# Gram products traced at the head of a step, and one PSUM group for branch B's output

## The chip, the cores and the metric

The kernel runs on one core of a Trainium2 chip. Its time is the device time of one execution in microseconds; it was taken in three runs, and the median counts. Five engines work side by side, each through its own list of instructions in a fixed order: TensorE (PE) multiplies, VectorE (DVE) and ScalarE (ACT) do elementwise work and copy results out of PSUM, GpSimd (POOL) does some of the elementwise work, and SyncE (SP) issues the DMAs. An instruction waits until what it reads has been written and what it overwrites has been read.

## The reference

One decoder block over 1040 tokens of width 1024 (16 meta tokens and 1024 of the sequence), all in float32: a half-step feed-forward (FFN1), two sequence mixers A and B on the same normalized input, their gated sum through an output projection, a second feed-forward (FFN2). This change concerns the mixers.

- A is a gated DeltaNet with 8 heads of width 128. In chunks of 64 tokens in the reference: `m = strict(kb @ k.T * decay)`, `tinv = inv(m + I)`, `u = tinv @ vb`, `wk = tinv @ (kb * exp(g))`, `attn = (q @ k.T) * decay`, and then a chain over the chunks, `v_new = u - w @ state`, `o = qg @ state + attn @ v_new`, `state = state * exp(gl) + kt.T @ v_new`.
- B is an RWKV-7 recurrence with 16 heads of width 64, token by token in the reference:

```
sa = einsum('bhvk,bhk->bhv', state, a_t)
state = state * w_t + sa * b_t + v_t * k_t
y_t = einsum('bhvk,bhk->bhv', state, r_t)
```

The kernel computes B in chunks too: products of decayed keys and queries inside a chunk (Gram products), the inverse of a triangular matrix, and a state handed from chunk to chunk. Then `o_a` and `o_b` are normalized, gated and added.

## The kernel before

The program has three parts: FFN1 (0 to some 790 us), the mixers (to some 2300 us), and the output projection with FFN2. The mixers run in 16 steps: two segments of tokens (528 with the meta tokens, then 512), in each eight steps j, and a step handles head j of A and heads 2j and 2j+1 of B. A head of B has 64 rows, so B's matmuls are 64x64 and use one quadrant of the PE array each; HS are the two halves of 64 rows.

What a step consists of, as functions: `decay`, `new_b` and `new_a` make the inputs of a later step by the input projection (the matmuls pp, L307, three for each weight tile w, whose halves ACT L163 and DVE L164 prepare). `operands` (L1411) makes the Gram products: B's grb (L1428), masked into LT by DVE (L1431), and A's gra (L1467), from which DVE takes UA (L1471) and attn (L1473). It then sends LT and UA's diagonal blocks through DRAM (scr, L1548 and L1551) and loads them in another layout as Ub (L1557, L1559); transposes keys (bkt, L1498, into BKt) and AR (vp<-ck,AR, into at); computes B's output inside a chunk from older tokens (vp<-LT,Vs, copied by ACT into yb, L1515); and makes ktl and the scaled kq. `inverses` (L1562) inverts the small diagonal blocks in 62 serial DVE instructions (tb L1581, Xb L1583), copies the result (Yt, L1584) and sends it through DRAM. `merge_blocks` builds the whole inverse Y of them (iv). `transitions` (L1645) solves with Y (xp), and makes B's chunk transitions: xa, xv, vbk, mt, AR's second half and vbk's final form, with the PSUM tiles xp, vp, mp and np; the second part of np (np<-LT,xv) is B's output from the solved values, which DVE adds to yb (L1698). `chains` (L1701) runs both chains over the chunks (p, b, pq) and ends with bq (L1773), B's output from the states; DVE adds it to yb (L1775). `gates` and `finish` (L1808) normalize and merge; cs and bon (L1213) are their sums over rows of hl.

PSUM has eight banks: four for pp (mm), two for the operands (mx), two for transitions, chains and bq (ch). A tile waits for a bank of its pool until what stood in it has been copied out.

The order comes from a table of strings (L187 to L192), which says in which order the functions are traced: "+" is a function of the next step, "++" of the one after. A scheduler then puts the instructions of each engine into a fixed order; it prefers what was traced earlier among what its model takes to be ready. The steps of one segment have the same order on each engine but for buffers. Helper `run` (L1249, matmul L1266) issues 16 matmuls for each kind that it is given, over all four quadrants, into two banks of a pool.

Of the kernel before, what the change touches and what calls it, by code (L numbers as in the profile page):

```python
# [25 lines left out]
FULL = 512  # L26
CB = 64
NCB = FULL // CB
CA = 128
NCA = FULL // CA  # L30
# [3 lines left out]
HS = (slice(0, 64), slice(64, 128))  # L34
# [149 lines left out]

FIRST = "decay new_b tokens new_a decay+ operands inverses new_b+ new_a+"  # L187
REGULAR = "merge_blocks transitions operands+ inverses+ chains gates finish decay++ new_b++ new_a++"
BEFORE_SWITCH = "merge_blocks transitions operands+ inverses+ chains gates finish banks gates+ segment decay++ new_b++ tokens++ new_a++"
SWITCH = "merge_blocks transitions operands+ inverses+ chains finish decay++ new_b++ new_a++"  # L190
LAST_BUT_ONE = "merge_blocks transitions operands+ inverses+ chains gates finish"
FINAL = "gates merge_blocks transitions chains fill finish"  # L192


# [858 lines left out]
def ch3(ap, c):  # L1053
    return ap.rearrange("p (a b) -> p a b", b=c)
# [184 lines left out]
def tok(i, h):  # L1239

    return h ^ (i & 1)


def key(i, h):

    return 1 - tok(i, h)


def run(g, pool, name, *kinds):  # L1249


    ps, out, used = {}, [], [0, 0]
    for f in kinds:
        ds = [f(i, 0)[2] ^ f(i, 0)[3] for i in range(2)]
        at = []
        for d in ds:
            if d not in ps:
                ps[d] = pool.tile([P, 512], F32, name=name, tag=pool.name)
            at.append(used[d])
            used[d] += NCB // 2 * CB  # L1260
        for i in range(NCB):
            e, c0 = ds[i & 1], at[i & 1] + i // 2 * CB
            for h in range(2):
                l, r, src, dst = f(i, h)
                assert src ^ dst == e
                g.nc.tensor.matmul(ps[e][HS[dst], c0 : c0 + CB], lhsT=l, rhs=r, start=True, stop=True)  # L1266
        out.append([(ch3(ps[d][:, c0 : c0 + NCB // 2 * CB], CB), cs) for d, c0, cs in zip(ds, at, EO)])
    return out
# [139 lines left out]
        nc.scalar.activation(vkm[:, 0, :], ps[:16, 0:P], AF.Copy)  # L1408


def operands(g, q):  # L1411

    nc, st, V, c, j, n, off = g.nc, g.st, g.V, q.c, q.j, q.n, q.off
    meta = q.s == 0
    fs = slice(off, off + FULL)
    tmp = lambda name, w=528: tmp_tile(g, name, w)
    kq, AR, BK = q.kq, q.AR, q.BK
# [4 lines left out]
    LT = q.LT = st.tile([P, NCB, 2, P], F32, name="LT", tag="LT", bufs=2)  # L1422
    for c4 in range(0, NCB, 4):
        ps = [g.mx.tile([P, 512], F32, name="grb", tag="mx") for _ in range(2)]
        for i in range(4):
            for d in range(2):
                for h in range(2):
                    nc.tensor.matmul(ps[d][HS[h ^ d], i * P : (i + 1) * P], lhsT=BK[HS[h], c4 + i, d ^ (i & 1)],  # L1428
                                     rhs=AR[HS[h], c4 + i].rearrange("p a b -> p (a b)"), start=True, stop=True)
# [3 lines left out]
    if meta:  # L1433
        nc.vector.tensor_copy(g.bkpm[0:64, 0, :], g.bkm[0:64, :])
        nc.vector.tensor_copy(g.bkpm[64:128, 1, :], g.bkm[64:128, :])
        ps = g.mx.tile([P, 512], F32, name="gbm", tag="mx")
        for h in range(2):
# [3 lines left out]
                                op=ALU.mult)  # L1441


    E = ch3(tmp("E", 512), CA)
    kts = st.tile([P, NCA], F32, name="kts", tag="kts")
# [9 lines left out]
    eg = gp  # L1455
    nc.scalar.activation(eg, gp, AF.Exp)
    nc.scalar.activation(kts, kts, AF.Exp)
    egl = q.egl = st.tile([P, NCA], F32, name="egl", tag="egl", bufs=2)
    nc.gpsimd.tensor_copy(egl.unsqueeze(2), ch3(eg, CA)[:, :, CA - 1 : CA])
    attn = q.attn = st.tile([P, NCA, CA], F32, name="attn", tag="attn", bufs=2)  # L1460
    UA = q.UA = st.tile([P, NCA, CA], F32, name="UA", tag="UA", bufs=1)
    for b in range(2):
        ps = g.mx.tile([P, 512], F32, name="gra", tag="mx")
        for c2 in range(2):
            i = 2 * b + c2
            tsl = slice(off + i * CA, off + (i + 1) * CA)
            nc.tensor.matmul(ps[:, c2 * 256 : c2 * 256 + 256], lhsT=kq[:, 0, tsl], rhs=kq[:, :, tsl],  # L1467
                             start=True, stop=True)
# [5 lines left out]
    if meta:  # L1474
# [3 lines left out]
        em = q.em = st.tile([16, 3, 16], F32, name="em", tag="em", bufs=2)  # L1478
# [10 lines left out]

    inverse_inputs(g, q)  # L1490

    BKt = q.BKt = st.tile([P, NCB, 2, CB], F32, name="BKt", tag="BKt")
    ident = g.C("ident")
    ps = [g.mx.tile([P, 512], F32, name="bkt", tag="mx") for _ in range(2)]
    for i in range(NCB):
        for d in range(2):
            for h in range(2):
                nc.tensor.matmul(ps[d][HS[h ^ d], i * CB : (i + 1) * CB], lhsT=BK[HS[h], i, d ^ (i & 1)],  # L1498
                                 rhs=ident[HS[h], HS[h]], start=True, stop=True)
    for d in range(2):  # L1500
        nc.scalar.activation(BKt[:, :, d], ch3(ps[d], CB), AF.Copy)

    Vs = q.Vs
    at = q.at = st.tile([P, NCB, CB], F32, name="at", tag="at")
    yb = q.yb = st.tile([P, FULL], F32, name="yb", tag="yb", bufs=2)

    def vr(i, h):
        k = key(i, h)
        return Vs[HS[k], i], LT[HS[k], i, 1 - (i & 1), CB:], k, h

    pa, pr = run(g, g.mx, "vp", lambda i, h: (AR[HS[h], i, 0, :], ident[HS[h], HS[h]], h, tok(i, h)), vr)
    for ps, cs in pa:
        nc.scalar.activation(at[:, cs], ps, AF.Copy)
    for ps, cs in pr:
        nc.scalar.activation(ch3(yb, CB)[:, cs], ps, AF.Copy)  # L1515
# [6 lines left out]
    ps = g.mx.tile([P, 512], F32, name="ktp", tag="mx")  # L1522
# [3 lines left out]
    if meta:  # L1526
        vkm = q.vkm
        ps = g.mx.tile([P, 512], F32, name="vmp", tag="mx")
# [76 lines left out]
def merge_blocks(g, q):  # L1605

    nc, st = g.nc, g.st
    LT, UA, Xc, XA = q.LT, q.UA, q.Xc, g.XA
    Y = g.Y[q.it % 2]
# [32 lines left out]
    nc.vector.tensor_copy(Y[0:64, NCB:, 64:128], ch3(ps4[0:64, 0:256], 64))  # L1642


def transitions(g, q):  # L1645

    nc, st = g.nc, g.st
    Y = g.Y[q.it % 2]
    AR, LT, BKt, Vs, yb = q.AR, q.LT, q.BKt, q.Vs, ch3(q.yb, CB)
    vbk = q.vbk = st.tile([P, NCB, CB], F32, name="vbk", tag="vbk")  # L1650
    xa, xv = (st.tile([P, NCB, CB], F32, name=x, tag=x) for x in ("xa", "xv"))

    vka = q.at
# [12 lines left out]

    def va(i, h):
        k = key(i, h)
        return LT[HS[k], i, 1 - (i & 1), :CB], Vs[HS[k], i], k, 1 - k

    def vb(i, h):
        k = key(i, h)
        return BKt[HS[k], i, 1 - (i & 1)], Vs[HS[k], i], k, h

    px, pv = run(g, g.ch, "xp", solved(q.at), va)
    for ps, cs in pv:
        nc.scalar.activation(vka[:, cs], ps, AF.Copy)
    for ps, cs in px:
        nc.scalar.activation(xa[:, cs], ps, AF.Copy)
    for ps, cs in run(g, g.ch, "xp", solved(vka))[0]:  # L1680
        nc.scalar.activation(xv[:, cs], ps, AF.Copy)
    for ps, cs in run(g, g.ch, "vp", vb)[0]:
        nc.scalar.activation(vbk[:, cs], ps, AF.Copy)
    bt = lambda r, i: BKt[r, i, i & 1]
    br = lambda r, i: LT[r, i, i & 1, CB:]
    pm, pr = run(g, g.ch, "mp", by_tok(lambda r, i: xa[r, i], bt), by_tok(lambda r, i: xa[r, i], br))
    for ps, cs in pm:
        for hp in HS:
            nc.vector.tensor_tensor(g.mt[hp, cs, hp], ps[hp], g.C("ident")[hp, hp].unsqueeze(1).to_broadcast([CB, NCB // 2, CB]),  # L1689
                                    op=ALU.add)  # L1690
    for ps, cs in pr:
        nc.vector.tensor_tensor(AR[:, cs, 1, :], ps, AR[:, cs, 1, :], op=ALU.add)
    pn, py = run(g, g.ch, "np", by_tok(bt, lambda r, i: xv[r, i]), by_tok(lambda r, i: xv[r, i], br))
    for ps, cs in pn:
        nc.vector.tensor_tensor(vbk[:, cs], ps, vbk[:, cs], op=ALU.add)
    nc.vector.tensor_tensor(vbk, vbk, q.gam.unsqueeze(2).to_broadcast([P, NCB, CB]), op=ALU.mult)
    for ps, cs in py:
        nc.vector.tensor_tensor(yb[:, cs], ps, yb[:, cs], op=ALU.add)  # L1698


def chains(g, q):  # L1701

    nc, st, c, j = g.nc, g.st, q.c, q.j
    meta = q.s == 0
# [6 lines left out]
    if meta:  # L1711
        ym, ltm, uvm = q.ym, q.ltm, g.uvm[q.it % 2]
        ps = pt("bm1")
# [4 lines left out]
        ps = pt("bm2")  # L1718
# [3 lines left out]
        ps = pt("bm3")  # L1722
# [4 lines left out]
        ps = pt("am1")  # L1727
# [3 lines left out]
        ps = pt("am2")  # L1731
# [27 lines left out]
    SBs = st.tile([P, NCB + 1, CB], F32, name="SBs", tag="SBs")  # L1759
# [9 lines left out]
        chunk_a(i)  # L1769
    ps = pt("bq")  # L1770
    for i in range(NCB):
        for hp in HS:
            nc.tensor.matmul(ps[hp, i * CB : (i + 1) * CB], lhsT=SBs[hp, i], rhs=q.AR[hp, i, 1, :],  # L1773
                             start=True, stop=True)
# [33 lines left out]
def finish(g, q):  # L1808
# [17 lines left out]
    else:  # L1826
        g.mg.append(u_tile(g, yb))


ACTIONS = {"new_b": new_b, "tokens": tokens, "new_a": new_a, "operands": operands, "inverses": inverses, "merge_blocks": merge_blocks, "transitions": transitions,  # L1830
           "chains": chains,
           "gates": gates, "finish": finish, "fill": fill}

# [85 lines left out]
```

## Time and profile before

| what | value |
|---|---|
| time, median of three runs | 3006.02 us (3003.01 to 3011.42) |
| the profiled execution | 3009.62 us, span 3007.6 us |
| mean granted PE clock | 0.99 of full speed |
| PE, DVE, ACT, POOL busy | 96%, 73%, 48%, 16% of the span |
| one step, first segment | 94.0 us, of which PE is busy 90.8 |
| one step, second segment | 86.9 us, of which PE is busy 83.8 |

A row of a timeline gives start, length, engine, source line, operation, output<-inputs, shapes and number of instructions; in brackets stand the idle time just before it and what ended it. A wait row says which engine and line waited for which, then the total in us, the number of times and the longest. A row by line gives number, busy time, mean ns of one, and idle time before. A 64x64 or 128x128 fp32 matmul is recorded as two instructions, so that 16 matmuls are 32 records; pp, whose operands are split into two halves beforehand, is one record each. Each time in the text is of the profiled execution unless the median is named.

### The profile page before, as it was taken

Reading aid. Unit: us, or ns where it says so; the run is one execution under the profiler, and the core shown is the slowest. Engines: PE = TensorE matmul, PEld = TensorE weight load, DVE = VectorE, ACT = ScalarE, POOL = GpSimd, SP = SyncE. Lnnn points to the kernel's source line nnn. Section 1 sums busy time; section 2 is a strip of 40 time slices with the busy share of each in tenths; the row PEclk is TensorE's granted clock in tenths of the full one; section 3 lists DMA queues with packets and bytes.
Section 4 is the critical chain, followed back from the end, with each engine's and each line's share of the span. In section 5 each row is a group of like instructions: output and inputs, shape, how many; then the busy total and the mean of one; then the engine's idle time right before and its main releaser. Section 6 shows DMA issues by size and latency. Waiting matters only on the chain.

```text
span 3007.6 us, 62829 instructions
## 1 busy us (share of the span) xinstructions
PE 2890.0 (96%) x25630; PEld 2501.7 (83%) x25630; DVE 2194.8 (73%) x4079; ACT 1445.0 (48%) x2546; POOL 491.2 (16%) x554
## 2 busy tenths in 40 slices
PE   8999999998989999999998999999998999999998
PEld 8999999998878888888776777777776888888886
DVE  7566668776667877788767887777866666667886
ACT  5322234345655656566566656656644432223444
POOL 0332332323000000000000100100100033332531
PEclk9999999999999999999999999999999999999999
DMA  3433236453232322333332332233354333333762
GB/s 123 134 107 106 93 122 210 170 193 111 74 74 66 83 72 64 81 82 87 93 90 71 81 82 75 74 84 86 106 148 158 114 109 103 100 104 132 248 226 95
DMA packets 286849, 333.14 MB, mean 111 GB/s; under 512 B 172432, under 2 KB 178576, under 8 KB 286560
## 3 DMA queue, kind: packets, MB, share of 16 engines
q1 hardware_dynamic: 284752, 325.77, 35.7%
q8 instruction: 201, 3.29, 0.5%
q10 hardware_dynamic: 1728, 3.16, 0.3%
q14 instruction: 88, 0.72, 0.1%
q0 software_dynamic: 80, 0.19, 0.0%
HBM read 261.67 MB, written 67.38 MB: 109 GB/s over the span
## 4 chain that ended last, share of the span: by engine, by line
PE 50%; DVE 12%; ACT 5%; issue 2%; DMA 1%; SPq 0%; POOL 0%; DVEq 0%; ACTq 0%
PE pp L307 16%; PE pg L494 11%; PE pd L707 6%; PE pwo L307 3%; DVE w L164 2%; DVE tb L1581 1%; PE pg L518 1%; DVE Xb L1583 1%; ACT w L163 1%; PE cs L1213 1%; PE vp L1266 1%; PE mp L1266 1%; DVE mt L1689 1%; PE gra L1467 1%; PE np L1266 1%
## 5 line engine op out<-in xcount | busy, mean ns | idle before, releaser
L307 PE MATMUL pp<-uk,w 128*128 128x512 f32 (+2 forms) x4824 | 969.8, 347 | 15.2 <-DVE h L714 6.0
L307 PEld LDWEIGHTS pp<-uk,w 128*128 128x128 f32 x4824 | 744.0, 191 | 111.9 <-DVE w L164 13.1
L707 PE MATMUL pd<-form,w 128*128 128x256 f32 (+2 forms) x2772 | 437.2, 320 | 9.9 <-DVE w L164 9.2
L707 PEld LDWEIGHTS pd<-form,w 128*128 128x128 f32 x2772 | 396.7, 190 | 49.9 <-DVE w L164 12.3
L494 PE MATMUL pg<-bt,w 128*128 128x256 f32 (+2 forms) x2520 | 401.7, 318 | 2.5 <-DVE w L164 2.0
L164 DVE TENSOR_TENSOR w<-wraw,w 128x1024 fp32r<-128x1024 f32 (+2 forms) x266 | 349.2, 1313 | 74.9 <-ACT w L163 71.8
L494 PEld LDWEIGHTS pg<-bt,w 128*128 128x128 f32 x2520 | 360.2, 188 | 36.4 <-DVE w L164 3.1
L163 ACT ACTIVATE w<-wraw 128x1024 fp32r<-128x1024 f32 (+2 forms) x266 | 276.5, 1040 | 191.5 <-PE pg L494 116.1
L500 DVE TENSOR_TENSOR c<-c,pg 128x520 f32<-128x520 f32 (+1 forms) x280 | 189.5, 689 | 240.0 <-PE pg L494 216.0
L494 PE MATMUL pg<-b,w 128*128 128x256 f32 (+2 forms) x2160 | 347.9, 318 | 0.0
L494 PEld LDWEIGHTS pg<-b,w 128*128 128x128 f32 x2160 | 309.8, 188 | 28.0
L163 ACT ACTIVATE w<-wrx 128x1024 fp32r<-128x1024 f32 (+1 forms) x64 | 58.4, 912 | 280.4 <-PE pg L494 238.5
L464 POOL TENSOR_TENSOR wrx<-wrx 128x512 f32<-128x512 f32 x38 | 52.5, 1382 | 727.0 <-DVE w22b L164 549.8
L164 DVE TENSOR_TENSOR form<-form 128x520 fp32r<-128x520 f32 (+1 forms) x152 | 145.1, 991 | 13.0 <-ACT form L163 12.7
L163 ACT ACTIVATE w<-wsum 128x768 fp32r<-128x768 f32 x96 | 75.7, 788 | 160.3 <-PE pd L707 120.9
L164 DVE TENSOR_TENSOR w<-wsum,w 128x768 fp32r<-128x768 f32 x96 | 116.0, 1214 | 36.8 <-ACT w L163 36.8
L1583 DVE TENSOR_TENSOR Xb<-Xb,tb 115x126 f32<-115x126 f32 (+22 forms) x496 | 125.8, 254 | 8.9 <-DVE tb L1581 0.2
L163 ACT ACTIVATE form<-form 128x520 fp32r<-128x520 f32 (+1 forms) x152 | 94.2, 632 | 77.1 <-DMA form<-frm 67.7
L1581 DVE TENSOR_TENSOR tb<-Ub,Xb 115x126 f32<-115x126 f32 (+22 forms) x496 | 124.5, 251 | 8.4 <-DMA Ub<-scr 1.2
L242 POOL TENSOR_TENSOR wsum<-wsum,wraw 128x768 f32<-128x768 f32 (+1 forms) x48 | 96.3, 2020 | 209.7 <-DMA wraw<-in_wdn 122.1
L1390 DVE SCALAR_TENSOR_TENSOR acc<-xr,pk,acc 128x528 f32<-128x528 f32 (+1 forms) x144 | 108.9, 757 | 28.5 <-ACT acc L1386 28.0
L307 PE MATMUL pwo<-uk,w 128*128 128x512 f32 x384 | 99.5, 412 | 4.1 <-DVE w L164 1.9
(424 smaller groups left out, 4391.3 us busy)
## 6 DMA issues: line engine op xcount, KB each, us to landing
wraw<-in_win SPq DMA_DIRECT2D x150, 512.0 KB
wraw<-in_wgu SPq DMA_DIRECT2D x44, 512.0 KB
wrx<-in_wgu SPq DMA_DIRECT2D x44, 512.0 KB
frm<-c SPq DMA_DIRECT2D x76, 260.0 KB
form<-frm SPq DMA_DIRECT2D x76, 260.0 KB
frm<-c SPq DMA_DIRECT2D x76, 256.0 KB
form<-frm SPq DMA_DIRECT2D x76, 256.0 KB
wraw<-in_wdn SPq DMA_DIRECT2D x40, 384.0 KB
```

The source lines that it names most:

```text
L163: g.nc.scalar.activation(hi, src, AF.Copy)
L164: (eng or g.nc.vector).tensor_tensor(lo, src, hi.bitcast(F32), op=ALU.subtract)
L242: g.nc.gpsimd.tensor_tensor(s, x, y, op=ALU.add if r == 1 else ALU.subtract)
L307: g.nc.tensor.matmul(ps, lhsT=l, rhs=r, start=i == 0, stop=i == n - 1)
L464: sums.tensor_tensor(a22, a21, a22, op=ALU.add)
L494: nc.tensor.matmul(ps[:, c0 : c0 + cn], lhsT=l[:, x, k, :], rhs=r[:, k, y, c0 : c0 + cn], start=i == 0, stop=i == 3 * HK - 1)
L500: nc.vector.tensor_tensor(o, x, y, op=ALU.add)
L707: nc.tensor.matmul(pd[:, c0 : c0 + cn], lhsT=wd[:, u, k - k0, :], rhs=x[:, v, c0 : c0 + cn], start=k + i == 0, stop=k == HF - 1 and i == 2)
L1266: g.nc.tensor.matmul(ps[e][HS[dst], c0 : c0 + CB], lhsT=l, rhs=r, start=True, stop=True)
L1390: nc.vector.scalar_tensor_tensor(acc[:, :n], xr[:, tap : tap + n], V("convw", ct * 4 + tap), acc[:, :n], op0=ALU.mult, op1=ALU.add)
L1581: nc.vector.tensor_tensor(tv, U[:, i, i + 1 :].unsqueeze(2).to_broadcast([npt, nt, ncc]), X[:, i, 0:ncc].unsqueeze(1).to_broadcast([npt, n ...
L1583: nc.vector.tensor_tensor(X[:, i + 1 :, 0:ncc], X[:, i + 1 :, 0:ncc], tv, op=ALU.add)
```

## The change

`operands` is cut into two functions. `grams` makes LT, the decay matrix E, attn and UA, em, and the inversion's loads; `operands` keeps BKt, at, ktl, the scaled kq and the state loads. In the table, the next step's `grams` stands at the head of a step, ahead of `merge_blocks` of the step itself; `operands` stays behind `transitions`. UA gets two buffers, yb one.

B's output is summed differently. The products vp<-LT,Vs in `operands` and np<-LT,xv in `transitions`, 16 matmuls each, are sorted anew by the half of rows that they read. Those whose source half differs from the half they write (16) form yp at the end of `transitions`, in one bank, copied by one ACT copy of 128x512 to yb. Those with the same half (16) are put into bq's PSUM group: each block of the bank gets a matmul with start and then bq's own matmul, which adds to it. The final DVE addition of bq to yb stays; the two additions of L1698 go.

```diff
-REGULAR = "merge_blocks transitions operands+ inverses+ chains gates finish decay++ new_b++ new_a++"
+REGULAR = "grams+ merge_blocks transitions operands+ inverses+ chains gates finish decay++ new_b++ new_a++"
...
-def operands(g, q):
+def grams(g, q):
...
-    UA = q.UA = st.tile([P, NCA, CA], F32, name="UA", tag="UA", bufs=1)
+    UA = q.UA = st.tile([P, NCA, CA], F32, name="UA", tag="UA", bufs=2)
...
     inverse_inputs(g, q)
 
+
+def operands(g, q):
...
-    yb = q.yb = st.tile([P, FULL], F32, name="yb", tag="yb", bufs=2)
-
-    def vr(i, h):
-        k = key(i, h)
-        return Vs[HS[k], i], LT[HS[k], i, 1 - (i & 1), CB:], k, h
-
-    pa, pr = run(g, g.mx, "vp", lambda i, h: (AR[HS[h], i, 0, :], ident[HS[h], HS[h]], h, tok(i, h)), vr)
+    pa, = run(g, g.mx, "vp", lambda i, h: (AR[HS[h], i, 0, :], ident[HS[h], HS[h]], h, tok(i, h)))
     for ps, cs in pa:
         nc.scalar.activation(at[:, cs], ps, AF.Copy)
-    for ps, cs in pr:
-        nc.scalar.activation(ch3(yb, CB)[:, cs], ps, AF.Copy)
...
+def tokens_of(q, i, h, r):
+
+    src, odd = (q.xv, i & 1) if r == tok(i, h) else (q.Vs, 1 - (i & 1))
+    return src[HS[r], i], q.LT[HS[r], i, odd, CB:]
...
-    pn, py = run(g, g.ch, "np", by_tok(bt, lambda r, i: xv[r, i]), by_tok(lambda r, i: xv[r, i], br))
-    for ps, cs in pn:
+    for ps, cs in run(g, g.ch, "np", by_tok(bt, lambda r, i: xv[r, i]))[0]:
         nc.vector.tensor_tensor(vbk[:, cs], ps, vbk[:, cs], op=ALU.add)
     nc.vector.tensor_tensor(vbk, vbk, q.gam.unsqueeze(2).to_broadcast([P, NCB, CB]), op=ALU.mult)
-    for ps, cs in py:
-        nc.vector.tensor_tensor(yb[:, cs], ps, yb[:, cs], op=ALU.add)
+    yb = q.yb = st.tile([P, FULL], F32, name="yb", tag="yb")
+    ps = g.ch.tile([P, 512], F32, name="yp", tag="ch")
+    for i in range(NCB):
+        for h in range(2):
+            l, r = tokens_of(q, i, h, 1 - h)
+            nc.tensor.matmul(ps[HS[h], i * CB : (i + 1) * CB], lhsT=l, rhs=r, start=True, stop=True)
+    nc.scalar.activation(yb, ps, AF.Copy)
...
     for i in range(NCB):
-        for hp in HS:
-            nc.tensor.matmul(ps[hp, i * CB : (i + 1) * CB], lhsT=SBs[hp, i], rhs=q.AR[hp, i, 1, :],
-                             start=True, stop=True)
+        for h, hp in enumerate(HS):
+            o = ps[hp, i * CB : (i + 1) * CB]
+            l, r = tokens_of(q, i, h, h)
+            nc.tensor.matmul(o, lhsT=l, rhs=r, start=True, stop=False)
+            nc.tensor.matmul(o, lhsT=SBs[hp, i], rhs=q.AR[hp, i, 1, :], start=False, stop=True)
     nc.vector.tensor_tensor(q.yb, ps, q.yb, op=ALU.add)
```

How the orders change is shown at three places. In a row stand the line, the operation, output<-inputs, the shape of the result and how many follow each other; the line numbers of the new program differ by up to 12 for the same instruction. First PE in the transitions of a step of the second segment, before, from mp on:

```order
L1266 MATMUL mp<-BKt,xa 64x64 x16
L1266 MATMUL mp<-LT,xa 64x64 x16
L1428 MATMUL grb<-AR,BK 64x128 x16
L1467 MATMUL gra<-kq 128x256
L1266 MATMUL np<-xv,BKt 64x64 x16
L1266 MATMUL np<-LT,xv 64x64 x16
L1467 MATMUL gra<-kq 128x256 x3
L1498 MATMUL bkt<-ck,BK 64x64 x16
```

and now:

```order
L1266 MATMUL mp<-BKt,xa 64x64 x16
L1266 MATMUL mp<-LT,xa 64x64 x16
L1506 MATMUL bkt<-ck,BK 64x64 x11
L1266 MATMUL vp<-ck,AR 64x64 x8
L307 MATMUL pp<-uk,w 128x512 x3
L1266 MATMUL vp<-ck,AR 64x64 x2
L1266 MATMUL np<-xv,BKt 64x64 x16
L1266 MATMUL vp<-ck,AR 64x64 x6
L307 MATMUL pp<-uk,w 128x512
L1707 MATMUL yp<-LT,Vs 64x64 x2
```

Between mp and np stand bkt, vp and pp in place of grb and gra, which now come ahead of the last iv; in the first segment it is thirty bkt. Second, DVE in the same step. Before, the inversion's end stands right ahead of rB:

```order
L1583 TENSOR_TENSOR Xb<-Xb,tb 115x2x15
L1581 TENSOR_TENSOR tb<-Ub,Xb 115x16
L1583 TENSOR_TENSOR Xb<-Xb,tb 115x16
L1127 SCALAR_TENSOR_TENSOR rB<-pp,pk,rB 128x512
L1584 COPY Yt<-Xb 115x512
L1360 TENSOR_TENSOR AR<-rB,ELx 128x8x64
```

Now its end stands in `finish`, five rows and more ahead of rB, and its beginning between AR and vbk in `transitions`:

```order
L1698 TENSOR_TENSOR AR<-mp,AR 128x4x64 x2
L1580 TENSOR_TENSOR tb<-Ub,Xb 115x31
L1582 TENSOR_TENSOR Xb<-Xb,tb 115x31
L1580 TENSOR_TENSOR tb<-Ub,Xb 115x30
L1582 TENSOR_TENSOR Xb<-Xb,tb 115x30
L1580 TENSOR_TENSOR tb<-Ub,Xb 115x58
L1700 TENSOR_TENSOR vbk<-np,vbk 128x4x64 x2
```

Before, the first tb came behind ktl, kq and the chains' first instructions; in the first segment it now comes behind vbk. Third, PE at the change of segment, before:

```order
L1213 MATMUL cs<-hl,bdr 128x512
L307 MATMUL pp<-uk,w 128x512 x3
L1213 MATMUL bon<-hl,bdr 128x512
L307 MATMUL pp<-uk,w 128x512 x2
L1213 MATMUL bon<-hl,bdr 128x512
L307 MATMUL pp<-uk,w 128x512 x25
```

and now:

```order
L1213 MATMUL cs<-hl,bdr 128x512
L307 MATMUL pp<-uk,w 128x512 x44
L1213 MATMUL bon<-hl,bdr 128x512
L307 MATMUL pp<-uk,w 128x512 x4
L1213 MATMUL bon<-hl,bdr 128x512
L307 MATMUL pp<-uk,w 128x512 x12
```

Matmuls pp that stood behind the two bon stand ahead of them.

More of the change, by code (lines that the diff above doesn't have):

```diff
@@ L183, in schedule @@
                 yield act.rstrip("+"), it + act.count("+")
-FIRST = "decay new_b tokens new_a decay+ operands inverses new_b+ new_a+"
-REGULAR = "merge_blocks transitions operands+ inverses+ chains gates finish decay++ new_b++ new_a++"
-BEFORE_SWITCH = "merge_blocks transitions operands+ inverses+ chains gates finish banks gates+ segment decay++ new_b++ tokens++ new_a++"
-SWITCH = "merge_blocks transitions operands+ inverses+ chains finish decay++ new_b++ new_a++"
-LAST_BUT_ONE = "merge_blocks transitions operands+ inverses+ chains gates finish"
+FIRST = "decay new_b tokens new_a decay+ grams operands inverses new_b+ new_a+"
+REGULAR = "grams+ merge_blocks transitions operands+ inverses+ chains gates finish decay++ new_b++ new_a++"
+BEFORE_SWITCH = "grams+ merge_blocks transitions operands+ inverses+ chains gates finish banks gates+ segment decay++ new_b++ tokens++ new_a++"
+SWITCH = "grams+ merge_blocks transitions operands+ inverses+ chains finish decay++ new_b++ new_a++"
+LAST_BUT_ONE = "grams+ merge_blocks transitions operands+ inverses+ chains gates finish"
 FINAL = "gates merge_blocks transitions chains fill finish"
@@ L1444, in operands @@
     E = ch3(tmp("E", 512), CA)
-    kts = st.tile([P, NCA], F32, name="kts", tag="kts")
+    kts = q.kts = st.tile([P, NCA], F32, name="kts", tag="kts")
     gp = tmp("gp", FULL)
@@ L1490, in operands @@
     inverse_inputs(g, q)
+def operands(g, q):
+    nc, st, c, j, off = g.nc, g.st, q.c, q.j, q.off
+    meta = q.s == 0
+    fs = slice(off, off + FULL)
+    kq, AR, BK, kts, eg, em = q.kq, q.AR, q.BK, q.kts, q.eg, meta and q.em
     BKt = q.BKt = st.tile([P, NCB, 2, CB], F32, name="BKt", tag="BKt")
@@ L1648, in transitions @@
     Y = g.Y[q.it % 2]
[L1649 removed]
+    AR, LT, BKt, Vs = q.AR, q.LT, q.BKt, q.Vs
     vbk = q.vbk = st.tile([P, NCB, CB], F32, name="vbk", tag="vbk")
     xa, xv = (st.tile([P, NCB, CB], F32, name=x, tag=x) for x in ("xa", "xv"))
+    q.xv = xv
     vka = q.at
```

5 lines of the change are left out of this document (2 added, 3 removed).

## The prediction

> **What bounds the kernel now.** I read the first part of the page, then stretches of single steps, then who PE waited for.
>
> ```profile
> span 3007.6 us, 62829 instructions
> PE 2890.0 (96%) x25630; PEld 2501.7 (83%) x25630; DVE 2194.8 (73%) x4079; ACT 1445.0 (48%) x2546; POOL 491.2 (16%) x554
> ```
>
> PE is busy for 96% of the span, so time can only be won from PE's waits or from PE's own work. Next, one step of each segment (columns: stretch, length, busy time and instructions of each engine, granted clock, DMA share, GB/s), and the 24 us around the change of segment:
>
> ```profile
> 1149.30:1243.31 94.01, 90.82 (x1126) 78.96 (x1126) 72.91 (x181) 55.48 (x116) 4.51 (x22) 1.00 0.30 76
> 1882.04:1968.91 86.87, 83.80 (x941) 66.86 (x940) 70.42 (x167) 52.82 (x102) 7.91 (x15) 1.00 0.32 84
> 1601.00:1625.00 24.00, 15.97 (x60) 11.62 (x59) 23.41 (x60) 12.43 (x19) 1.59 (x4) 0.86 0.10 37
> ```
>
> A step holds 3.2 us of PE idle time in the first segment (94.01 less 90.82) and 3.1 in the second. At the change of segment PE idles 8.0 us, DVE is busy for 23.41 of 24 us, and a clock of 0.86 means another 24 x 0.14 = 3.4 us lost. PE's waits in the mixers, 800 to 2300 us (total us, times, longest):
>
> ```profile
> PE bon L1213 <- ACT hl L163: 17.4, 12, 7.6
> PE xp L1266 <- ACT at L1677: 9.8, 14, 1.1
> PE np L1266 <- DVE AR L1692: 8.5, 14, 1.0
> PE cs L1213 <- ACT hl L1227: 4.2, 3, 3.1
> PE vp L1266 <- ACT xv L1681: 3.6, 15, 0.3
> PE iv L1616 <- DMA Xc<-scX: 1.9, 1, 1.9
> PE bm L1715 <- DVE yb L1698: 1.1, 5, 0.2
> ```
>
> That is all there is to win, some 46 us of 3007. Why bon waits in a step of the second segment:
>
> ```profile
> 1959.85 0.69 ACT L1126 ACTIVATE rB<-pp,pk 128x512 f32<-128x512 f32 x1 [3.07 <-PE pp L307]
> 1961.61 0.17 DVE L1583 TENSOR_TENSOR Xb<-Xb,tb 115x16 f32<-115x16 f32 x1
> 1961.70 0.74 DVE L1127 SCALAR_TENSOR_TENSOR rB<-pp,pk,rB 128x512 f32<-128x512 f32 x1
> 1962.36 0.61 DVE L1584 COPY Yt<-Xb 115x512 f32<-115x512 f32 x1
> 1968.92 0.75 DVE L1362 SCALAR_TENSOR_TENSOR bv<-rB,pk,kB 128x512 f32<-128x512 f32 x1
> 1970.39 0.50 PE L1213 MATMUL bon<-hl,bdr 128*128 128x512 f32 x1 [1.48 <-ACT hl L163]
> ```
>
> ACT's half of rB ends at 1960.54, but DVE first ends the previous inversion and starts rB 1.16 us later; Yt then stands in the chain to bv too.
>
> **The change part by part.** *Matmuls.* Their number stays: of the 48 per step for B's output (16 vp<-LT,Vs, 16 np<-LT,xv, 16 bq), 16 become yp and 16 join bq's group. Where they run changes. Each fp32 matmul is two records:
>
> ```profile
> 2007.48 0.97 PE L1498 MATMUL bkt<-ck,BK 64*64 64x64 f32 x26
> 2008.24 0.27 PE L1266 MATMUL vp<-ck,AR 64*64 64x64 f32 x2
> 2008.92 0.63 PE L1266 MATMUL vp<-LT,Vs 64*64 64x64 f32 x30
> 2009.49 0.66 PE L1524 MATMUL ktp<-ck,kq 128*128 128x128 f32 x4
> ```
>
> bkt, on two quadrants of the array, starts 26 records in 0.76 us, 29 ns each; vp, on four, 30 in 0.57 us, 19 ns each. The change takes away 64 records at 19 ns (1.22 us); yp and the new half of bq's group use two quadrants each, so 64 records at 29 ns (1.86 us). That is +0.64 us a step, over 16 steps **+10.2 us**, on the bound engine. Bounds: 0, if yp overlaps its neighbours on the other quadrants, and +0.94 a step (+15), if it overlaps nothing and pays an entry and an exit, which follow from bq:
>
> ```profile
> 2023.64 0.48 PE L307 MATMUL pp<-uk,w 128*128 128x512 f32 x1
> 2024.06 1.15 PE L1773 MATMUL bq<-AR,SBs 64*64 64x64 f32 x32
> 2025.13 1.20 PE L307 MATMUL pp<-uk,w 128*128 128x512 f32 x4
> 1981.74 3.13 PE L307 MATMUL pp<-uk,w 128*128 128x512 f32 x13
> 1984.71 0.39 PE L1213 MATMUL cs<-hl,onesr 128*128 128x512 f32 x1
> ```
>
> A pp takes 2.97 / 13 = 0.23 us; the one ahead of bq holds the place for 0.42, so 0.19 to change to small tiles; bq takes 1.07 for 32 x 29 ns = 0.93, so 0.14 to change back: 0.33 us a visit.
>
> *Visits.* PE's order has 26 changes of tile size in a step of the first segment and 20 in the second; with the change 32 and 24, so three and two visits more. At 0.33 us that is 0.99 and 0.66, over eight steps each +13; at nothing, 0. I take half, since several visits lie next to 128x128 matmuls that had a change beside them already: **+6.5 us**. The Trainium skill (TensorEngine Tiling (Array Packing), Key Properties) says that changing the tiling mode, not just the tile, drains TensorE. The row of bq agrees, with its 0.33 us; by the rule alone every visit pays in full.
>
> *Gram products in longer runs.*
>
> ```profile
> L1428 PE MATMUL grb<-AR,BK 64*64 64x128 f32 x896 | 54.5, 280 | 1.1 <-issue 1.0
> 1999.94 1.49 PE L1428 MATMUL grb<-AR,BK 64*64 64x128 f32 x28
> 2001.37 0.70 PE L1467 MATMUL gra<-kq 128*128 128x256 f32 x2
> ```
>
> 64 records take 54.5 / 14 = 3.9 us a step; a run of 28 goes at 1.43 / 28 = 51 ns, 3.3 for 64. Between 0 and -0.6 a step I take -0.2: **-3 us** in 14 steps.
>
> *Waits that go.* The inversion's loads are issued half a step earlier, so its serial DVE work begins behind AR instead of in the chains and ends in finish, ahead of rB. Then bv follows rB's ACT half at 1960.54 without Yt: 1.16 + 0.54 = 1.7 us earlier, more than the 1.48 of bon's wait. All but the 7.6 of bon's row goes, less a rest at the change of segment: **-9 us** (bounds 0 and -9.8). xp's wait for its first half's eviction gets grb or bkt into the gap: **-8** of 9.8. cs and bm: **-2.5**, the 3.1 at the mixers' end staying.
>
> *Waits that grow.* np waits for mt and AR:
>
> ```profile
> 2000.08 1.73 DVE L1689 TENSOR_TENSOR mt<-mp,ck 64x256 f32<-64x256 f32 x4 [1.35 <-PE mp L1266]
> 2001.82 0.76 DVE L1692 TENSOR_TENSOR AR<-mp,AR 128x256 f32<-128x256 f32 x2
> 2002.39 0.96 PE L1266 MATMUL np<-xv,BKt 64*64 64x64 f32 x30 [0.32 <-DVE AR L1692]
> ```
>
> Those 2.5 us were covered by grb (1.43) and gra (0.7). Now bkt, vp and three pp stand there: 11 x 2 x 29 ns + 10 x 2 x 19 ns + 0.7 = 1.7; in the first segment thirty bkt, 1.74. So about 0.25 us a step more: **+3.6** (bounds 0 and +8).
>
> yp is new. It writes a PSUM bank of the pair that np uses, so it waits for the first vbk eviction; in the second segment DVE's queue has AR, then five inversion instructions, then vbk, and the first of those waits for Ub:
>
> ```profile
> 1992.61 0.50 PE L1640 MATMUL iv<-Y,T 64*64 64x64 f32 x5
> 2006.67 0.60 DVE L1471 SCALAR_TENSOR_TENSOR UA<-gra,tk,E 128x128 f32<-128x128 f32 x2
> 2008.49 2.63 SPq L1551 DMA_DIRECT2D scr<-UA  x4
> 2012.24 0.78 SPq L1557 DMA_DIRECT2D Ub<-scr  x2
> 2016.29 0.18 DVE L1581 TENSOR_TENSOR tb<-Ub,Xb 115x31 f32<-115x31 f32 x1
> ```
>
> From UA's end (2007.27) to the first tb pass 9.0 us. AR ends at 2002.58, which is 10 us after the last iv begins. With the change gra stands right ahead of that iv, and UA ends about 1.5 us after it begins; Ub is then there at 1.5 + 9 = 10.5, as late as AR or half a microsecond later. I take 0.5 us of yp wait in seven steps, **+3.5** (bounds 0 and, with Ub 2 us later still and vbk behind the five instructions, 3.5 us a step, +24).
>
> *Change of segment.* There bon waits 7.61 us while DVE is full. The new order puts 44 pp where 3 stood ahead of bon, 41 x 0.23 = 9.4 us of cover, and one w of DVE earlier; the second w comes just ahead of bv, so I keep some 3 us of the stall: -4.6, and half of the 3.4 us of clock: **-6.3** (bounds 0 and -11).
>
> *Nothing.* Two ACT copies (400 ns each) become one, and two DVE additions go:
>
> ```profile
> L1515 ACT ACTIVATE yb<-vp x32: 392/400/410, 810.3 to 2184.3; 128x256 f32<-128x256 f32 x32
> L1698 DVE TENSOR_TENSOR yb<-np,yb x32: 414/418/423, 889.7 to 2262.1; 128x256 f32<-128x256 f32 x32
> ```
>
> DVE wins 0.84 us a step, of which 21 us of 94 are idle; PE's work covers both. Without that cover it would be -13 us. Step 0 and the end have single waits of 1.9 and 3.1 us, which the new order can move either way: 0, within 5.
>
> Sum: 10.2 + 6.5 - 3 - 9 - 8 - 2.5 + 3.6 + 3.5 - 6.3 = -5.0 us. The profiled execution took 3009.62 us, 3.6 above the median of 3006.02, so 3004.6 there and **3001 us** beside the median.
>
> **The rivals.** *All waits go.* With Ub early enough, np as before, and 7.6 + 3.4 us at the change of segment: 10.2 + 6.5 - 3 - 9.8 - 9.8 - 2.5 - 11 = -19.4, about **2987**. For it: every one of these waits has its cause in an order that changes. Against it: DVE's 23.41 busy of 24 us.
>
> *PE pays in full.* Each visit at 0.33 us, yp at its upper bound: +6.5 and +5, so **3012**, or 3007 with the visits alone; the waits won are eaten by PE's own work. The 3007 is what the Trainium skill's rule above gives. For it: PE is the bound and yp stands between pp. Against: 26 visits a step are paid today in 90.8 us of which they are a small part. In effect this is also the case that the move does nothing.
>
> *The inversion takes DVE from the transitions* (the other side). In the second segment a late Ub holds vbk in DVE's queue; behind vbk wait yp, then on PE every chain matmul and pp. It costs from the point where Ub lands more than half a microsecond behind AR; beyond 0.7 us more in each of seven steps it eats the forecast's gain. At 3.2 us a step, 7 x 2.7 = 19 more than forecast: **3020**. For it: the 9.0 us from UA to tb, and a 512 KB w load that the new order puts into SP's queue ahead of Ub. Against it: tb at 2016.29 also had chain work ahead of it in DVE, so Ub may land sooner.
>
> **How the numbers follow.** A change of 0.3% (9 us) is about what can be told from none. Forecast 0.42, from 2993 to 3009: a third of it faster, the rest same. All waits go 0.25, faster. PE pays in full 0.13, mostly same. DVE's queue 0.20, slower but for a little. So faster 0.14 + 0.25 = 0.39, same 0.26 + 0.10 + 0.01 = 0.37, slower 0.02 + 0.03 + 0.19 = 0.24. The range, 2976 to 3020, takes in the rivals' own times and some 10 us below the fast one; the forecast's own is 2993 to 3009.
>
> **What would show it.** Right: bon's wait in the second segment gone, xp's small, PE busy longer by about 0.8 us a step in spite of the same matmuls, bq's group near 2.0 us. Wrong: a DVE wait of tb for Ub between AR and vbk with yp waiting in PE; np's wait over 1 us; pp waiting for w where 44 of them stand ahead of bon; bq's group far from 2 us, which would break the count by quadrants.

## The result and the profile after

The changed kernel takes 3035.63 us (median of four runs, 3033.54 to 3040.01). Runs of before, on the same chip, gave a median of 3008.72 us. The ratio is 1.0084, with a 95% interval from 1.0067 to 1.0102: the change makes the kernel slower by some 25 us. The forecast was 3001 us, in a range from 2976 to 3020; it was wrong, and on the wrong side.

Shown first are two lines of the changed kernel's page, and then one step of each segment (from the matmul group bq at the end of a step to that of the next), with the columns of before:

```profile
span 3032.4 us, 62721 instructions
PE 2917.1 (96%) x25630; PEld 2529.9 (83%) x25630; DVE 2184.2 (72%) x4047; ACT 1445.4 (48%) x2530; POOL 472.2 (16%) x554
```

```profile
1289.23:1386.03 96.80, 92.71 (x1130) 80.28 (x1130) 72.41 (x180) 56.04 (x116) 5.09 (x22) 1.00 0.30 74
1872.73:1960.39 87.66, 85.45 (x944) 68.64 (x944) 69.28 (x165) 52.55 (x101) 5.73 (x15) 1.00 0.31 81
```

PE has the same 25630 matmul records and is busy for 2917 instead of 2890 us. The 25 us of span are time in which PE is busy, not time in which it waits; a part of that busy time is at a lower granted clock, as the account of the prediction shows. A step of the first segment is 2.8 us longer (96.80 after 94.01), one of the second 0.8 us (87.66 after 86.87). PE's waits in the mixers, 800 to 2330 us:

```profile
PE np L1266 <- DVE AR L1698: 11.7, 13, 1.5
PE cs L1213 <- ACT hl L1227: 7.2, 4, 3.7
PE pp L307 <- DVE w L164: 6.6, 4, 4.2
PE grb L1428 <- DVE LT L1431: 6.5, 7, 1.0
PE yp L1707 <- DVE vbk L1700: 5.4, 5, 2.1
PE vap L1402 <- DVE acc L1394: 3.3, 10, 0.4
PE bon L1213 <- ACT hl L163: 2.7, 7, 0.6
PE iv L1634 <- DVE XA L1630: 2.3, 2, 1.7
PE xp L1266 <- ACT at L1683: 1.3, 5, 0.3
```

bon fell from 17.4 to 2.7 us and xp from 9.8 to 1.3: these waits went, as forecast. But np grew from 8.5 to 11.7, cs from 4.2 to 7.2, and grb (6.5, which had waited 1.0 in all) and yp (5.4) are new. All idle time of PE in the mixers, added up from the records, is 71.7 us before (780 to 2300 us) and 69.5 after (780 to 2330 us): what was won came back in other places.

Where PE's work grew can be seen by taking, for each record, the time from its start to the start of the next one, less idle time. In the mean of three equal steps, us a step (in brackets the number of records):

```
                 first segment          second segment
                 before     after       before     after
whole step       94.04      96.73       86.92      87.46
idle              3.21       4.12        2.96       1.98
the rest         90.83      92.61       83.96      85.48
  np<-LT,xv       0.66 (32)   -          0.62 (32)   -
  vp<-LT,Vs       0.60 (32)   -          0.60 (32)   -
  yp               -         0.83 (32)    -         1.08 (32)
  bq<-LT           -         0.99 (32)    -         0.99 (32)
  bq<-AR          1.08 (32)  1.08 (32)   1.08 (32)  1.08 (32)
  xp, all         2.57 (96)  3.45 (96)
  vp<-Vs,BKt      0.92 (32)  1.27 (32)
  vp<-ck,AR       0.78 (32)  0.72 (32)   0.58 (32)  1.32 (32)
  grb             2.82 (64)  2.47 (64)   2.94 (64)  2.70 (64)
```

B's output costs 0.56 us more in the first segment (0.83 + 0.99 - 1.26) and 0.85 in the second. That is about what was forecast (0.64). The rest of the growth, 1.2 and 0.7 us, is in matmuls that the change only moved: xp and vp<-Vs,BKt in the first segment, vp<-ck,AR in the second.

### The profile page after: what moved, and what is told of

Its sections match the earlier page's. It is cut to its first block, busy times and chain, and to the rows that moved or that the text cites. A ratio compares the mean times of both kernels' runs of the same rounds, so it can differ in the third digit from the quotient of the medians.

```text
span 3032.4 us, 62721 instructions
## 1 busy us (share of the span) xinstructions
PE 2917.1 (96%) x25630; PEld 2529.9 (83%) x25630; DVE 2184.2 (72%) x4047; ACT 1445.4 (48%) x2530; POOL 472.2 (16%) x554
## 4 chain that ended last, share of the span: by engine, by line
PE 71%; DVE 12%; ACT 6%; DMA 4%; issue 4%; SPq 1%; POOL 1%; DVEq 0%; ACTq 0%; POOLq 0%
PE pg L494 24%; PE pp L307 19%; PE pd L707 9%; PE pg L518 3%; PE pwo L307 3%; DVE w L164 2%; ACT w L163 1%; DVE form L164 1%; PE xp L1266 1%; PE cs L1213 1%; DMA form<-frm 1%; DMA Ub<-scr 1%; PE b L1774 1%; DVE acc L1390 1%; DVE tb L1580 1%
```

## The experiments

**The two halves of the change apart.** The first kernel (e_output) keeps the new way of summing B's output and puts the Gram products back behind transitions, in all four tables that the change altered for a step:

```diff
-REGULAR = "grams+ merge_blocks transitions operands+ inverses+ chains gates finish decay++ new_b++ new_a++"
+REGULAR = "merge_blocks transitions grams+ operands+ inverses+ chains gates finish decay++ new_b++ new_a++"
```

The second (e_order) keeps the new place of the Gram products, with the lines of before for vp, np, bq and yb. Two yb buffers and two of UA don't fit together, so UA has one, and `grams` stands right behind `merge_blocks`:

```diff
-REGULAR = "grams+ merge_blocks transitions operands+ inverses+ chains gates finish decay++ new_b++ new_a++"
+REGULAR = "merge_blocks grams+ transitions operands+ inverses+ chains gates finish decay++ new_b++ new_a++"
...
-    UA = q.UA = st.tile([P, NCA, CA], F32, name="UA", tag="UA", bufs=2)
+    UA = q.UA = st.tile([P, NCA, CA], F32, name="UA", tag="UA", bufs=1)
```

> Only the new way of summing B's output, with the Gram products back at their old place in the order (behind transitions, ahead of the other operands). Theory Q (the output's matmuls on two quadrants instead of four are what costs, about 1.7 us of PE in each of 16 steps): 20 to 28 us above before. Rival O (the new order costs, by np's and grb's waits and by more changes of tile size): within 6 us of before.

> Only the new order, with the old way of summing B's output (two yb buffers; to make room UA has one, so the Gram products stand right behind merge_blocks instead of ahead of it). Theory Q: within 8 us of before, since waits go in the second segment and come in the first. Rival O: 18 to 28 us above before.

Measured: e_output 1.0042 (1.0026 to 1.0059), e_order 1.0038 (1.0019 to 1.0056). Neither theory alone holds: each half costs 11 to 13 us, and 0.42 and 0.38% add up to 0.80 of the 0.84% measured. The order, from which I expected a gain, costs by itself. The two profiled executions cost in different ways. In e_output PE is busy for 2910.6 us (2890.0 before). In e_order it is busy for 2888.9, no more than before, but np waits 18.4 us in all for AR (8.5 before), and DVE's tb 18.6 us for Ub (1.2 before). The order of e_order is not quite that of the changed kernel, so its price need not be made up in the same way there.

**The output moved to four quadrants, in the new order.** One kernel (e_quad) issues all 32 products of LT together at the end of transitions over the four quadrants into two banks, and bq is that of before:

```diff
-    ps = g.ch.tile([P, 512], F32, name="yp", tag="ch")
+    ps = [g.ch.tile([P, 512], F32, name="yp", tag="ch") for _ in range(2)]
...
+            for d in range(2):
+                l, r = tokens_of(q, i, h, h ^ d)
+                nc.tensor.matmul(ps[d][HS[h], i * CB : (i + 1) * CB], lhsT=l, rhs=r, start=True, stop=True)
+    nc.scalar.activation(yb, ps[0], AF.Copy)
+    nc.vector.tensor_tensor(yb, ps[1], yb, op=ALU.add)
```

The other (e_inter) takes yp out of transitions and puts its matmuls between those of bq's group, into a bank py, which ACT then copies to yb:

```diff
             nc.tensor.matmul(o, lhsT=l, rhs=r, start=True, stop=False)
+            l, r = tokens_of(q, i, h, 1 - h)
+            nc.tensor.matmul(py[hp, i * CB : (i + 1) * CB], lhsT=l, rhs=r, start=True, stop=True)
```

> The changed kernel's order, but all 32 products of LT with Vs and xv are issued together at the end of transitions over all four quadrants into two banks (one ACT copy, one DVE addition), and bq's group is the plain 16 matmuls again. Theory Q: yp's 32 matmuls take about 1.2 us instead of 1.08 for 16, bq's group falls from 2.06 to 1.07 us; some 16 us below the changed kernel, 5 to 13 us above before. Rival O: within 6 us of the changed kernel.

> The changed kernel's order; the cross-half products (yp) leave transitions and are issued between the matmuls of bq's group, into a second bank, so that all four quadrants are in use there. Theory Q: the group stays at about 2.1 us and yp's own 1.1 us and its visit of 0.3 go: 18 to 22 us below the changed kernel, 2 to 8 us above before. If matmuls of other quadrants don't run beside the group's, it grows to some 3 us and the time stays within 6 us of the changed kernel, which is also what rival O expects.

Measured: e_quad 1.0096 (1.0072 to 1.0119), e_inter 1.0119 (1.0104 to 1.0134). Both are misses: neither is faster than the changed kernel. The waits say why, of e_quad first (800 to 2340 us):

```profile
PE yp L1708 <- DVE vbk L1700: 5.7, 5, 2.2
PE b L1776 <- DVE yb L1710: 4.6, 6, 1.5
DVE tb L1580 <- DMA Ub<-scr: 10.2, 8, 2.6
```

and of e_inter:

```profile
PE cs L1213 <- ACT yb L1784: 11.3, 11, 1.6
PE p L1742 <- DVE vbk L1700: 7.3, 5, 2.7
DVE tb L1580 <- DMA Ub<-scr: 7.5, 5, 2.6
```

In e_quad yp and the chains' first matmul wait for vbk and yb, in e_inter cs waits for the late copy of yb. PE is busy for 2909.2 and 2908.2 us, 8 and 9 less than in the changed kernel, and idle for 12 and 19 us more. So matmul time was saved and given back in waits, several of which hang on the eviction, in an order in which DVE's inversion stands ahead of vbk. One part of the theory came true: in e_inter the 96 records of the mixed group take 2.1 to 2.2 us a step, about what 64 took, so matmuls on the other quadrants do run beside the group's.

**The price of the order without any of it.** The next two kernels leave all 32 products of LT out of B's output (it lacks the part from inside a chunk), once with the tables of e_output (e_none_old) and once in the new order (e_none_new):

```diff
-    yb = q.yb = st.tile([P, FULL], F32, name="yb", tag="yb")
-    ps = g.ch.tile([P, 512], F32, name="yp", tag="ch")
...
-            nc.tensor.matmul(o, lhsT=l, rhs=r, start=True, stop=False)
-            nc.tensor.matmul(o, lhsT=SBs[hp, i], rhs=q.AR[hp, i, 1, :], start=False, stop=True)
+            nc.tensor.matmul(ps[hp, i * CB : (i + 1) * CB], lhsT=SBs[hp, i], rhs=q.AR[hp, i, 1, :], start=True, stop=True)
-    nc.vector.tensor_tensor(q.yb, ps, q.yb, op=ALU.add)
+    yb = q.yb = st.tile([P, FULL], F32, name="yb", tag="yb")
+    nc.vector.tensor_copy(yb, ps)
```

> The order of before, with all 32 products of LT left out of B's output (yb is a copy of bq's bank alone, so the output lacks B's part from inside a chunk). Theory: they cost 1.26 us of PE a step in before (0.66 for np<-LT,xv and 0.60 for vp<-LT,Vs) and no more, so 16 to 22 us below before. If they also cost visits of the small tile size, 25 us and more below.

> The same without the products, in the new order (Gram products at the head). It gives the order's price where no yp and no longer bq stand in the way. Theory (order and output each cost by themselves, 11 and 13 us): 8 to 14 us above the old order without the products, that is 6 to 14 us below before. Rival (the order costs only with yp in it): within 4 us of the old order without the products.

Measured: e_none_old 0.9923 (0.9896 to 0.9950), e_none_new 0.9957 (0.9946 to 0.9969); medians 2985.98 and 2997.56 us. The old way of summing costs 24 us in the old order, between the two expectations (16 to 22 for its matmuls alone, 25 and more with visits). The order costs 11.6 us with no yp and no longer bq in the way, so it doesn't need them. In an equal step of the first segment, e_none_old first:

```profile
1187.03:1280.64 93.61, 90.30 (x1063) 78.60 (x1062) 72.76 (x180) 55.46 (x115) 6.27 (x22) 1.00 0.29 77
```

and e_none_new:

```profile
1191.04:1285.53 94.49, 91.22 (x1064) 78.81 (x1063) 71.70 (x179) 55.33 (x115) 5.92 (x22) 1.00 0.28 76
```

Both have the same matmuls and the same idle time (3.3 us), but PE is busy 0.92 us longer. Counted from the records, PE changes the tile size (between 128 rows of the array and fewer) 26 times a step in the one and 32 times in the other: three visits more, 0.3 us each if the whole growth is put down to them. It is a net growth: grb's records take 0.80 us less a step, those of xp, vp<-Vs,BKt and pp 2.0 us more. So the price fits the count, but it was not tested by itself. The changed kernel shows what such a visit looks like; here gbm (128x16) stands in the middle of xp:

```profile
1348.53 1.69 PE L1428 MATMUL grb<-AR,BK 64*64 64x128 f32 x32 [1.03 <-DVE LT L1431]
1350.05 0.75 PE L1266 MATMUL xp<-Vs,LT 64*64 64x64 f32 x18
1350.83 0.41 PE L1438 MATMUL gbm<-arm,bkpm 128*64 128x16 f32 x4
1351.16 0.68 PE L1266 MATMUL xp<-Vs,LT 64*64 64x64 f32 x14
1360.82 1.01 PE L1266 MATMUL np<-xv,BKt 64*64 64x64 f32 x32 [1.10 <-DVE AR L1698]
```

These 32 records of xp take 0.78 + 0.61 us. Before, they took 0.81 together, with 24 of them in one run whose next row starts 0.66 us later:

```profile
1336.10 0.87 PE L1266 MATMUL xp<-Vs,LT 64*64 64x64 f32 x24
```

The rows of the changed kernel also show the two waits that eat xp's gain: grb in one long run waits for DVE to empty LT's banks, and np for AR. In the second segment the explanation by visits does not hold: PE changes 20 times in e_none_old and 18 times in e_none_new, and its time without idle is still 0.75 us longer in steps at full clock. Most of that is vp<-ck,AR (1.32 after 0.78), split by pp and np; the rest I can't name.

**yp in a bank of the operands' pool.**

```diff
-    ps = g.ch.tile([P, 512], F32, name="yp", tag="ch")
+    ps = g.mx.tile([P, 512], F32, name="yp", tag="mx")
```

> The changed kernel with yp in a bank of the operands' pool, so that it does not wait for the eviction of np into vbk. Theory: yp's waits of 5.4 us in all go, and yp can follow np or vp without a pp between, up to one visit (0.33 us) a step less: 4 to 10 us below the changed kernel. If the two banks of the operands are the scarcer ones: no gain, or grb and bkt wait instead.

Measured: 1.0064 (1.0040 to 1.0088), 3028.80 us, some 6 us below the changed kernel by the ratios. That lies in the range expected, but the interval overlaps that of the changed kernel (1.0067 to 1.0102), so the gain isn't clear of noise. In the second segment yp now runs ahead of np, and no wait of it for vbk is left in the trace, though DVE's wait for Ub is (7.3 us in seven times).

**Where in the program the order costs.** One kernel (e_sw_old) gives the two steps at the change of segment, tables BEFORE_SWITCH and SWITCH, the old place of the Gram products, as in e_output. The other (e_seg0_old) does so in all steps 0 to 7, so that only the second segment has the new order:

```diff
-        order = {NJ - 2: BEFORE_SWITCH, NJ - 1: SWITCH, last - 1: LAST_BUT_ONE, last: FINAL}.get(it, REGULAR)
+        order = {NJ - 2: BEFORE_SWITCH, NJ - 1: SWITCH, last - 1: LAST_BUT_ONE, last: FINAL}.get(it, EARLY if it < NJ else REGULAR)
...
+EARLY = REGULAR.replace("grams+ merge_blocks transitions", "merge_blocks transitions grams+")
```

> The changed kernel, but the two steps at the change of segment (the tables BEFORE_SWITCH and SWITCH) keep the old place of the Gram products. If the order's price of some 11 us lies mostly there (8.7 us between bq of step 6 and bq of step 9 in the two kernels without the products): 6 to 10 us below the changed kernel. If it is spread over the steps, by more visits of the small tile size: 1 to 2 us below.

> The changed kernel with the old order in steps 0 to 7 and the new order in the steps of the second segment alone. If the new order is free of cost where bon's wait goes (second segment): like the kernel with the new output in the old order, 11 to 14 us above before, or some us below that. If the visits cost there too: 3 to 6 us above that kernel.

Measured: e_sw_old 1.0098 (1.0076 to 1.0121), e_seg0_old 1.0061 (1.0042 to 1.0081). The tables at the change of segment are not the cause: nothing is won by them. With the new order in the second segment alone it is 0.61%, against 0.42% for the new output in the old order. The difference, some 6 us, lies near my upper bound, but the intervals overlap. So it only suggests that the new order isn't free even where bon's wait goes. The waits of e_seg0_old (800 to 2340 us) show one that comes up in its place:

```profile
PE yp L1708 <- DVE vbk L1701: 8.8, 5, 2.6
DVE tb L1581 <- DMA Ub<-scr: 14.0, 6, 5.2
```

In the changed kernel one such place looks so in the timeline of DVE, of SP's queue and of PE, and then in stretches of 2 us, with the clock behind the busy times:

```profile
1760.05 0.76 DVE L1698 TENSOR_TENSOR AR<-mp,AR 128x256 f32<-128x256 f32 x2
1763.30 0.19 DVE L1580 TENSOR_TENSOR tb<-Ub,Xb 115x31 f32<-115x31 f32 x1 [2.50 <-DMA Ub<-scr]
1763.93 0.75 DVE L1700 TENSOR_TENSOR vbk<-np,vbk 128x256 f32<-128x256 f32 x2
...
1757.40 0.37 SPq L260 DMA_DIRECT2D wraw<-in_win  x1
1758.53 0.78 SPq L1556 DMA_DIRECT2D Ub<-scr  x2
...
1764.41 0.33 PE L1707 MATMUL yp<-LT,Vs 64*64 64x64 f32 x4 [2.09 <-DVE vbk L1700]
```

```profile
1760.00:1762.00 2.00, 1.63 (x49) 1.43 (x47) 0.79 (x3) 0.41 (x1) 0.00 (x0) 1.00 0.79 252
1766.00:1768.00 2.00, 2.00 (x10) 1.90 (x9) 1.43 (x4) 0.39 (x1) 0.00 (x0) 0.50 0.03 8
```

SP issues a 512 KB weight load just ahead of Ub; the DMA engines are 79% busy from 1760 to 1762; Ub comes 2.5 us after AR, vbk stands behind tb in DVE's queue, and yp, with all of PE behind it, waits for vbk. After the 2.09 us of idle the granted clock is 0.50 for some 3.4 us, which costs another 1.7. That the weight load makes Ub late wasn't tried by itself; it is what these rows suggest.

**The old order with four quadrants.** This kernel has the bank pair at the end of transitions, as e_quad has, in the old order; it was measured twice.

> The order of before, and all 32 products of LT together at the end of transitions over all four quadrants into two banks, one ACT copy and one DVE addition, bq plain. Theory (two quadrants and visits are the price): PE as in before, 0.9 us less of DVE and ACT that lies covered: within 6 us of before. Rival (a stretch at the end of transitions costs by its wait for vbk, whatever its quadrants): 10 us or more above before.

> The version that came out lowest of those with the whole computation (old order, the products of LT on four quadrants into two banks), taken again. If its 0.11% is real: a ratio of 0.997 to 0.999 with an interval below 1; if not, an interval around 1.

Measured: 0.9989 (0.9973 to 1.0005), then 0.9982 (0.9971 to 0.9993), medians 3005.69 and 3003.27 us. In the old order the stretch doesn't wait for vbk, and the version is not slower than before. In the second, larger measurement it is faster by 0.18%, some 5 us. Its page:

```profile
span 3001.8 us, 62831 instructions
PE 2889.4 (96%) x25630; PEld 2503.6 (83%) x25630; DVE 2188.3 (73%) x4063; ACT 1449.8 (48%) x2530; POOL 488.6 (16%) x554
```

PE's busy time is that of before. The same products in groups on two quadrants (e_output, 3021.03 us) cost 15 to 18 us more than in one on four, in the same order. The traces of e_output and of the second measurement say where. From bq of step 1 to bq of step 6 the two lie close (477.0 and 474.5 us); from there to bq of step 8, over the change of segment, it is 211.1 and 202.6, and on to bq of step 14 it is 526.1 and 516.9. So the count of quadrants alone, which is the same in every step, isn't the whole cause.

Nor is the price of the order one number. It is 0.34% without the products (e_none_new against e_none_old), 0.42% with the change's output (the changed kernel against e_output), and 1.1% with the products on four quadrants (e_quad against e_old_quad).

## Why the prediction was wrong

*Where the sum failed.* The forecast was -5.0 us, and the profiled span grew by 24.8. The step that failed is that of the waits. Those that go (-19.5), those that grow (+7.1) and the stall at the change of segment (-4.6) made -17.0 us; PE's idle time, span less busy time, fell by 2.3 (117.6 to 115.3). The second is the work: matmuls, visits and longer runs made +13.7, and it grew by 20.2. The third is the clock: it was forecast at -1.7, and it cost 6.9 us more (PE was busy at a granted clock of 0.50 for 40.2 us before and for 53.9 after, and half of that is lost). These are sums over one execution of each.

*What bounds the kernel.* Right in the main: PE's work and PE's waits counted, and the clock beside them. The 46 us of waits were not all that there was; PE's idle time in the mixers was 71.7. The error was to look for the gain in waits and to price the visits at half.

*Matmuls, +10.2 us.* Right in mechanism and near in size (its upper bound was added up a little low: 0.64 + 0.33 is 0.97 a step, not 0.94). yp and bq's group in the changed kernel, in a step of the second segment (of the first yp's rows, the last ones and what follows):

```profile
1941.56 0.33 PE L1707 MATMUL yp<-LT,Vs 64*64 64x64 f32 x4 [0.44 <-DVE vbk L1700]
1942.42 0.28 PE L1707 MATMUL yp<-LT,xv 64*64 64x64 f32 x4
1942.64 0.66 PE L1523 MATMUL ktp<-ck,kq 128*128 128x128 f32 x4
...
1960.23 0.34 PE L1785 MATMUL bq<-LT,xv 64*64 64x64 f32 x4
1962.03 0.33 PE L1786 MATMUL bq<-AR,SBs 64*64 64x64 f32 x4
1962.29 0.73 PE L1213 MATMUL cs<-hl,onesr 128*128 128x512 f32 x2
```

yp takes 1.08 us and the group 2.06 for 64 records, near the 2.0 that was named (before, bq's 32 took 1.07, so accumulating into the same place costs nothing extra here). The whole output half measured 0.42%, 12.6 us. That this is near 10.2 is in part luck: by place, e_output's loss against four quadrants lies at the change of segment and in the second segment, and the term was meant for every step.

*Visits, +6.5 us.* Too small for the first segment. Half the price was taken because many visits would have a neighbour that changes anyway. In the first segment the count fits about 0.3 us each, nearly the full price of bq's row. The Trainium skill (TensorEngine Tiling (Array Packing), Key Properties) says that a change of tiling mode drains TensorE. The 0.28 to 0.31 us a visit agrees with it. The second segment's extra PE time isn't explained by the count of changes.

*Gram products in longer runs, -3 us.* The matmul time fell as said (0.35 and 0.24 us a step). What the term left out is that a run of 32 records fills both banks and then waits for DVE's LT: 1.03 us a step in the first segment. It was counted as a gain and is a loss in the first segment; the wait stands in the rows of the changed kernel above.

*Waits that go.* They went, and more fully than I said: -14.7 for bon (the stall at the change of segment included; 2.7 us stay) and -8.5 for xp. This is the step that misled: the waits were taken as time won, when the work that filled the gaps was missing elsewhere, as grb was ahead of np. np +3.2 (forecast +3.6) and yp 5.4 (forecast 3.5) came near what was said. grb, cs (+3.0), iv and vap (+1.6) were not foreseen. In all, PE's idle time in the mixers fell by 2.2 us.

*Change of segment, -6.3 us.* Wrong. bon's stall went, but DVE is just as full, and the next matmul that needs it waits instead (the wait in the timeline, then 13 us of busy times):

```profile
1647.84 0.50 PE L1213 MATMUL cs<-hl,onesr 128*128 128x512 f32 x1 [3.70 <-ACT hl L1227]
```

```profile
1637.00:1650.00 13.00, 9.07 (x73) 6.63 (x73) 13.00 (x24) 9.72 (x18) 2.88 (x3) 0.97 0.79 141
```

DVE is busy for 13.00 of 13 us. The 23.41 of 24 us of before stood in the prediction, as the argument against the rival in which all waits go; it spoke against this term too. The granted clock fell here as well: it is 0.50 from 1650 to 1656 us, behind the wait of cs. From bq of step 6 to bq of step 8 the changed kernel takes 212.8 us, after 202.6; some 4.6 of the difference are 20 more matmuls of 128x512 that now stand in this stretch (20 x 0.23). And the 3.4 us of clock were too many, since bon's wait lasted to 1618.4, into the 6.8 us at 0.50 that begin at 1615.1.

*The rivals.* "PE pays in full" fits the first segment, but its 3012 us kept the whole gain of the waits. "The inversion takes DVE from the transitions" is shown too, in some steps and not in all (tb waited for Ub six times, 8.4 us in all, at most 2.5); where it strikes, the clock can add to it. I had the two as alternatives, and both took place. Together they come near the measured time, but they do not make it up: with my own terms for the output (10.2) and the longer runs (-3), the visits at full price (13) and the waits at the -2 us measured, the sum is +18, and the 6.9 of the clock make it 25. This sum was made afterwards, with a price of visits that the second segment doesn't bear out, so that it comes out proves little.

*What stays open.* What makes PE's time without waits longer in the second segment beside vp<-ck,AR; and how the order's 11 to 12 us divide between the steps of the first segment, the change of segment and the second segment. The kernels that change one place have intervals too wide for that. The traces give only single executions: of the 24.8 us between the changed kernel and before, 10.1 lie ahead of bq of step 6, 10.3 from there to bq of step 8, and 4.4 behind it. That middle stretch takes 211.1 us in e_output and 203.5 in e_order, so much of what is lost there may come with the new output; but without the products the new order lengthens it too, from 200.1 to 206.1. Why either costs at that place wasn't tried.

## What to carry to other kernels

Here a wait that the order removed was not time won, because something else (DVE's evictions, PSUM banks, a DMA chain) was due almost as soon; add up the idle time that must remain before counting it as gain. Count how often a new order makes PE change its tile size and how many quadrants each group of small matmuls uses: fewer evictions were bought here with matmuls on two quadrants instead of four. When two rivals have different causes, ask also what they give together.

## What the runs showed of the hardware

A stall of PE of 2.09 us was followed by a granted clock of 0.50 for 3.4 us (1765.2 to 1768.6 us in the changed kernel), so this wait cost nearly twice its length. Its length alone doesn't tell: in before, a wait of 1.40 us (at 1457 us) was followed by 3.4 us at 0.50 too, while bon's waits of some 1.48 us in the second segment left the clock at 1.00. Matmuls that accumulate into the same PSUM block right behind each other ran as fast as ones that don't: 64 records on two quadrants took 2.06 us in the changed kernel, and 32 without accumulation 1.07 in before.
